# Taking a weight tile's scale from ScalarE's sums while VectorE inverts

## The chip, the cores and the metric

The kernel runs on one core of a Trainium2 chip. The metric is the device time of one execution in microseconds (us). Five engines of the core work side by side, each through its own queue in order: TensorE (PE, with weight loads as PEld), VectorE (DVE), ScalarE (ACT), GpSimd (POOL) and SyncE (SP, which issues most transfers).

## What is computed

One layer of a decoder trunk for a prompt of 1024 tokens and for 8 sample rows: an adaptive RMSNorm, one input projection of width 10368 from 2048 channels, two mixers and an output projection. The mixer that matters here is the RWKV-7 branch:

```
sa = S @ (-kk_t)
S  = S * d_t + sa * b_t + v_t * k_t        # for every token, per head of 64 channels
o  = S @ r_t
...
mixed = sigmoid(g_s5) * (o_s5 @ W_out[:D_S5]) + sigmoid(g_rw) * (o_rw @ W_out[D_S5:])
x = x + gate(c) * mixed
```

## The kernel before

**Products by jobs.** All large products are cut into jobs of 128 output channels (`run_jobs`). A job multiplies a weight tile of 2048 x 128 with the 1032 or 1040 columns of the activations, in three groups of some 344 columns. Operands are split into two float16 halves, a high and a low one, and three products of halves make one product, so a group is 3 x 16 = 48 matmuls (line 455) into one of three PSUM buffers `pg`. A group is read out by ACT and DVE: for a tile of the RWKV projections ACT writes a shifted copy `mt` (line 511) and DVE adds the two (line 517); for a gate branch `Z` the pair is lines 567 and 568. The buffer is free after DVE's part.

**Weight tiles.** Beside each job the next tile is prepared in three steps. `wload` fetches it as float32 into two buffers `ws` of 512 KB. `wscale` finds the largest magnitude: four searches of 128 x 512 each on DVE (`absmax`, the `wam` of line 157), a small one over their results (`wm`), a maximum over the partitions on POOL (`wg`), and five small DVE instructions that make a power of two of it (`wsc`, lines 147 to 151). `wsplit` then writes the high half `whi` on ACT (line 405) and the low half `wlo` on DVE (line 406), four times each. The fetch of the tile after next may start when the low halves are written.

**The recurrence.** The RWKV heads go in eight pairs (p = 0 to 7) through chunks of 64 tokens. For each pair `rw_operands` forms the chunk matrices, sends them through memory (`dA`), and `rw_tinv` inverts the 32 unit triangular matrices of a pair by elimination: 63 steps on DVE, each a product `TM` (line 800) and a subtraction that needs it (line 802). The results go to memory and back (`dT`, `TT`), and `rw_chain` walks over the 16 chunks with small matmuls on PE, the first of which that needs `TT` is `up` (line 835). `rw_side` transposes operands on DVE (line 770) and copies them on ACT (line 779).

**The order.** A hand-written planner (`Driver`) emits this background work between the matmuls of the jobs. Each generator yields its charge: nanoseconds of DVE, nanoseconds of PE, and a gap. The planner holds a clock for PE and one for DVE, and emits a step only while

```
b[1] <= self.pe and self.ve <= self.pe + self.slack
```

so what DVE is charged decides how many steps are emitted beside a job. A step of an inversion is charged `2 * (66 + n * m) / 0.96`, a search 600. Where a job needs a result, the planner is forced to emit up to it. The order of emission is a priority: a scheduler then lays instructions into the engines' queues, and sets later instructions between two that depend on each other.

PSUM buffers with the tag `pm` (two of them) serve the small products of the preparation, the tail and the operands; the inversions themselves use none.

Of the kernel before, what the change touches and what calls it, by code (L numbers as in the profile page):

```python
# [11 lines left out]
F32 = mybir.dt.float32  # L12
F16 = mybir.dt.float16
I32 = mybir.dt.int32
AF = mybir.ActivationFunctionType
# [51 lines left out]
class Driver:  # L67
# [6 lines left out]
    def __init__(self, slack=800.0):  # L74
        self.pe = 0.0
        self.ve = 0.0
        self.slack = slack
        self.bgs = []
# [52 lines left out]
class Hybrid:  # L131
    def __init__(self, ctx, tc, d):
        self.ctx, self.tc, self.nc, self.d = ctx, tc, tc.nc, d
        self.drv = Driver()
        self.scaled = False
        self.rotate = False
        self.flags = set()

# [236 lines left out]

    def wscale(self, job):

        n = len(job.ws)
        am = self.sm.tile([128, 4], F32, name="wam", tag="wam")
        for h in range(n):  # L380
            for q in range(2):
                self.absmax(am[:, 2 * h + q:2 * h + q + 1], job.ws[h][:, 4 * q:4 * q + 4, :], axis=mybir.AxisListType.XY)
                yield (600, 0, 0)
        m1 = self.sm.tile([128, 1], F32, name="wm1", tag="wm1")
        self.absmax(m1, am[:, :2 * n])
        g = self.sm.tile([128, 1], F32, name="wg", tag="wg")
        self.gmax(g, m1)
        yield (100, 0, WGAP)
        job.sc = self.sm.tile([128, 2, 1], F32, name="wsc", tag="wsc", bufs=3)
        self.pow2(g, job.sc)  # L390
        job.known = True
        yield (300, 0, 0)
# [398 lines left out]
    def rw_tinv(self, p):  # L791
        nc = self.nc
        TL = self.TL
        yield (0, 0, 5000)
        for k in range(63):
            n = k // 4 + 1
            m = 63 - k
            row = self.L1[:, k, k + 1:] if k < 32 else self.L2[:, k - 32, k - 31:]
            TM = self.TM[:, 0:n * m].rearrange("p (n m) -> p n m", m=m)
            nc.vector.tensor_tensor(out=TM, in0=row.unsqueeze(1).to_broadcast([128, n, m]),  # L800
                                    in1=TL[:, :n, k:k + 1].to_broadcast([128, n, m]), op=ALU.mult)
            nc.vector.tensor_tensor(out=TL[:, :n, k + 1:], in0=TL[:, :n, k + 1:], in1=TM, op=ALU.subtract)  # L802
            yield (2 * (66 + n * m) / 0.96, 0, 0)
        D4 = self.dT.rearrange("c h (j q) i -> q (c h) j i", q=4)
        for q in range(4):
            nc.sync.dma_start(D4[q], TL[32 * q:32 * q + 32])
        for e in range(2):
            for h in range(2):
                nc.sync.dma_start(self.TT[64 * e:64 * e + 64, :, 64 * h:64 * h + 64],
                                  self.dT[e::2, h].rearrange("c j i -> j c i"))  # L810
        yield (0, 0, 5500)
# [972 lines left out]
```

## Time and profile before

| | |
|---|---|
| median of 3 runs (lowest to highest) | 2981.96 us (2981.56 to 2985.08) |
| the profiled execution: its own time, its span | 2985.64 us, 2983.8 us |
| mean granted TensorE clock | 0.965 |
| PE busy, share of the span | 2726.1 us, 91% |
| DVE busy | 2031.8 us, 68% |
| ACT busy | 1102.7 us, 37% |
| DVE searches over weight tiles (`wam`) | 404, 267.7 us |

Busy time is the sum of an engine's instructions; it does not tell which of them the others waited for. The span is the time from the first to the last instruction. Matmuls overlap, so that one of them has a duration of some 0.31 us while a new one starts each 0.15 us.

### The profile page before, as it was taken

What the parts mean: (1) busy time and instruction counts of PE and PEld (TensorE: products, weight loads), DVE (VectorE), ACT (ScalarE), POOL (GpSimd) and SP (SyncE); (2) the same over time, 40 slices, a digit from 0 to 9 for tenths busy, and PEclk for the clock granted to TensorE, in tenths of its full rate; (3) what the DMA queues carried; (4) which work ended last, traced back from release to release, by engine and by line L of the source; (5) the groups of instructions that cost most, each with busy time, mean ns of one, the idle gap of its engine ahead of it and who ended that gap; (6) DMA issues with size and microseconds to landing.
All of it is one profiled execution on the core that took longest, in us unless ns stands there. A gap on an engine that the chain in (4) does not pass through costs nothing.

```text
span 2983.8 us, 47078 instructions
## 1 busy us (share of the span) xinstructions
PE 2726.1 (91%) x18330; PEld 1818.3 (61%) x18330; DVE 2031.8 (68%) x5106; ACT 1102.7 (37%) x1930; POOL 211.7 (7%) x426
## 2 busy tenths in 40 slices
PE   5699989999989999999899899999999897999997
PEld 1166656666656566666566566665666664666664
DVE  5579878754676756865857767667568855666665
ACT  2143223334434245254154253352442245522321
POOL 2100000010100100001001001000000000000002
PEclk7799999999999999999999999999999998999998
DMA  9734443331221222122212212222222347574443
GB/s 354 251 77 90 85 73 92 93 87 51 69 49 53 70 51 74 54 61 75 57 42 77 67 47 67 60 59 66 50 76 68 97 149 240 167 239 141 144 141 128
DMA packets 433582, 297.62 MB, mean 100 GB/s; under 512 B 115056, under 2 KB 399888, under 8 KB 432080
## 3 DMA queue, kind: packets, MB, share of 16 engines
q1 hardware_dynamic: 357136, 255.85, 30.5%
q10 hardware_dynamic: 76064, 38.47, 4.7%
q8 instruction: 144, 2.36, 0.3%
q14 instruction: 78, 0.64, 0.1%
q0 software_dynamic: 160, 0.30, 0.0%
HBM read 237.24 MB, written 57.32 MB: 99 GB/s over the span
## 4 chain that ended last, share of the span: by engine, by line
PE 28%; DVE 17%; DMA 10%; issue 6%; ACT 3%; POOL 1%; SPq 1%; ACTq 0%; DVEq 0%; POOLq 0%
PE pg L455 21%; DMA od<-BV 3%; DVE TM L800 3%; DVE ZB L802 3%; DMA ws<-w_in 3%; DVE wlo L406 2%; DVE wam L157 1%; PE pma L737 1%; DMA gw<-w_ada 1%; PE up L841 1%; PE sp L840 1%; DMA TT<-dT 1%; PE up L835 1%; PE xp L827 1%; PE xp L828 1%
## 5 line engine op out<-in xcount | busy, mean ns | idle before, releaser
L455 PEld LDWEIGHTS <-whi 128*128 128x128 f16 x9600 | 943.5, 99 | 550.2 <-issue 106.5
L455 PE MATMUL pg<-H,whi 128*128 128x344 f16 (+2 forms) x3840 | 1199.3, 312 | 60.9 <-DVE ZB L517 33.4
L455 PE MATMUL pg<-H,wlo 128*128 128x344 f16 (+2 forms) x3840 | 1199.4, 312 | 0.0
L455 PE MATMUL pg<-HL,whi 128*128 128x344 f16 (+2 forms) x3840 | 1199.1, 312 | 0.0
L455 PEld LDWEIGHTS <-wlo 128*128 128x128 f16 x4800 | 473.1, 99 | 236.7 <-issue 15.0
L405 ACT ACTIVATE whi<-ws,wsc 128x512 f16<-128x512 f32 x404 | 267.5, 713 | 374.7 <-PE pg L455 113.7
L157 DVE TENSOR_REDUCE wam<-ws 128x1 f32<-128x512 f32 x404 | 267.7, 679 | 146.8 <-DMA ws<-w_in 106.2
L406 DVE SCALAR_TENSOR_TENSOR wlo<-ws,wsc,whi 128x512 f16<-128x512 f32 x404 | 294.0, 748 | 42.1 <-ACT whi L405 40.6
L455 PE MATMUL pg<-OH,whi 128*128 128x344 f16 (+3 forms) x960 | 297.8, 311 | 10.4 <-ACT OH L1433 9.4
L455 PE MATMUL pg<-OLo,whi 128*128 128x344 f16 (+3 forms) x960 | 298.8, 311 | 4.0 <-DVE OLo L1435 2.7
L455 PE MATMUL pg<-OH,wlo 128*128 128x344 f16 (+3 forms) x960 | 298.8, 311 | 0.0
L800 DVE TENSOR_TENSOR TM<-ZB 128x252 f32<-128x252 f32 (+52 forms) x504 | 175.8, 349 | 78.4 <-DMA ZB<-dA 68.6
L802 DVE TENSOR_TENSOR ZB<-ZB,TM 128x252 f32<-128x252 f32 (+52 forms) x504 | 175.7, 349 | 10.2
L154 POOL PARTITION_ALL_REDUCE wg<-wm x105 | 47.1, 448 | 1459.4 <-DVE wm L157 1438.2
L236 PE MATMUL pmod<-wa,cs 128*32 128x512 f32 x256 | 76.2, 833 | 41.8 <-DMA wa<-w_ada 41.8
L830 ACT COPY XR<-xp 64x128 f32<-64x128 f32 x128 | 33.1, 259 | 219.7 <-DVE XS L829 219.2
L832 ACT ACTIVATE SG<-S,GC 128x128 f32<-128x128 f32 x120 | 48.0, 400 | 173.6 <-DVE S L843 134.5
L511 ACT ACTIVATE mt<-pg,rinv 128x347 f32<-128x347 f32 (+1 forms) x75 | 39.8, 538 | 139.0 <-PE pg L455 81.0
L835 PE MATMUL up<-XS,TT 128*128 128x128 f32 x256 | 56.3, 302 | 37.9 <-DMA TT<-dT 24.2
L1505 DVE SCALAR_TENSOR_TENSOR sg<-pg,oinv,sg 128x344 f32<-128x344 f32 (+3 forms) x96 | 54.9, 572 | 52.6 <-PE pg L455 52.4
L843 DVE SCALAR_TENSOR_TENSOR S<-sp,GC,SG 128x128 f32<-128x128 f32 x120 | 41.8, 348 | 69.5 <-PE sp L840 67.4
L701 ACT COPY BT<-ZB 64x128 f32<-64x128 f32 x256 | 75.7, 296 | 26.4 <-PE pma L737 17.6
(451 smaller groups left out, 3142.6 us busy)
## 6 DMA issues: line engine op xcount, KB each, us to landing
ws<-w_in SPq DMA_DIRECT2D x162, 512.0 KB
wa<-w_ada SPq DMA_DIRECT2D x64, 512.0 KB
sg<-sgd SPq DMA_DIRECT2D x32, 516.0 KB
gw<-w_ada ACTq DMA_DIRECT2D x32, 512.0 KB
ws<-w_out SPq DMA_DIRECT2D x32, 512.0 KB
XT<-xT SPq DMA_DIRECT2D x16, 516.0 KB
xo<-xT SPq DMA_DIRECT2D x16, 516.0 KB
ZB<-dA SPq DMA_DIRECT2D x8, 1024.0 KB
```

Source lines behind the costliest of these rows:

```text
L154: self.nc.gpsimd.partition_all_reduce(out, in_, 128, bass_isa.ReduceOp.absmax)
L157: self.nc.vector.tensor_reduce(out=out, in_=in_, axis=axis, op=ALU.max, apply_absolute_value=True)
L236: self.nc.tensor.matmul(q[s:s + 32], cs[:, kt, :], w[:, i, :], start=(kt < 4), stop=(kt >= 12))
L405: nc.scalar.activation(out=hi[:, ks, :], in_=s, func=AF.Copy, scale=job.sc[:, 0, 0:1])
L406: nc.vector.scalar_tensor_tensor(out=lo[:, ks, :], in0=s, scalar=job.sc[:, 0, 0:1], in1=hi[:, ks, :], op0=ALU.mult, op1=ALU.subtract)
L455: nc.tensor.matmul(q[:, :w], a[:, wk, :], b[:, rk, g0:g1], start=(n == 0), stop=(n == tot - 1))
L701: self.nc.scalar.copy(self.BT[k % 2][i][64 * h:64 * h + 64, :, 64 * h:64 * h + 64], t[64 * h:64 * h + 64, 128 * k:128 * k + 128].rearrange ...
L800: nc.vector.tensor_tensor(out=TM, in0=row.unsqueeze(1).to_broadcast([128, n, m]), in1=TL[:, :n, k:k + 1].to_broadcast([128, n, m]), op=ALU ...
L802: nc.vector.tensor_tensor(out=TL[:, :n, k + 1:], in0=TL[:, :n, k + 1:], in1=TM, op=ALU.subtract)
L832: nc.scalar.activation(out=self.SG, in_=S0, func=AF.Copy, scale=g)
L835: nc.tensor.matmul(up[:, 0, :], self.TT[:, a, :], xs, start=True, stop=True)
L1505: V.scalar_tensor_tensor(out=f, in0=q[:, :g1 - g0], scalar=job.inv[:, w:w + 1], in1=f, op0=ALU.mult, op1=ALU.mult)
```

## The change

While the 63 steps of an inversion are being emitted, a flag `inverting` is set. A weight tile whose `wscale` is emitted in that time no longer has its four searches on DVE. In their place stand four activations on ACT that write magnitudes to a PSUM buffer `pab`, which nobody reads, and whose accumulators give the sum of magnitudes along each row; the rest of the step goes on with sums in the place of maxima. The planner is charged 0 for them and not 600. Elsewhere the searches stay.

```
+        self.inverting = False
...
+                a, w = am[:, 2 * h + q:2 * h + q + 1], job.ws[h][:, 4 * q:4 * q + 4, :]
+                if self.inverting:
+
+                    o = self.ps.tile([128, 4, 128], F32, name="pab", tag="pm", bufs=2)
+                    nc.scalar.activation(out=o, in_=w, func=AF.Abs, accum_out=a)
+                    yield (0, 0, 0)
+                else:
+                    self.absmax(a, w, axis=mybir.AxisListType.XY)
+                    yield (600, 0, 0)
...
         yield (0, 0, 5000)
+        self.inverting = True
         for k in range(63):
...
             yield (2 * (66 + n * m) / 0.96, 0, 0)
+        self.inverting = False
```

## Rows read from the trace of the kernel before

**Rows 1.** The page's span, and part 1: busy time of each engine.

```profile
span 2983.8 us, 47078 instructions
PE 2726.1 (91%) x18330; PEld 1818.3 (61%) x18330; DVE 2031.8 (68%) x5106; ACT 1102.7 (37%) x1930; POOL 211.7 (7%) x426
```

**Rows 2.** Engines' busy us (and instructions): fifth inversion; sums over inversions; stretches after.

```profile
1606.00:1680.00 74.00, 67.81 (x453) 44.64 (x451) 64.06 (x187) 17.69 (x32) 6.79 (x16) 1.00 0.19 51
...
sum 582.00, PE 529.07 PEld 345.83 DVE 506.78 ACT 134.24 POOL 48.47; mean PE 66.13 PEld 43.23 DVE 63.35 ACT 16.78 POOL 6.06
...
sum 1066.00, PE 1006.32 PEld 703.04 DVE 647.63 ACT 501.61 POOL 68.25; mean PE 125.79 PEld 87.88 DVE 80.95 ACT 62.70 POOL 8.53
```

**Rows 3.** DVE's groups in the fifth inversion, 1606 to 1680 us.

```profile
L802 DVE TENSOR_TENSOR ZB<-ZB,TM 128x252 f32<-128x252 f32 (+52 forms) x63 | 21.9, 348 | 1.2
L800 DVE TENSOR_TENSOR TM<-ZB 128x252 f32<-128x252 f32 (+52 forms) x63 | 21.9, 348 | 8.6 <-DMA ZB<-dA 7.4
...
L157 DVE TENSOR_REDUCE wam<-ws 128x1 f32<-128x512 f32 x12 | 8.1, 678 | 0.9 <-DMA ws<-w_in 0.9
```

**Rows 4.** DVE in order of time, inside the fifth inversion.

```profile
1644.90 0.44 DVE L802 TENSOR_TENSOR ZB<-ZB,TM 128x280 f32<-128x280 f32 x1
1645.26 0.68 DVE L157 TENSOR_REDUCE wam<-ws 128x1 f32<-128x512 f32 x1
1645.86 0.43 DVE L800 TENSOR_TENSOR TM<-ZB 128x272 f32<-128x272 f32 x1
...
1650.37 0.44 DVE L800 TENSOR_TENSOR TM<-ZB 128x270 f32<-128x270 f32 x1
1650.84 0.44 DVE L802 TENSOR_TENSOR ZB<-ZB,TM 128x270 f32<-128x270 f32 x1
```

**Rows 5.** Instructions on `wam` between successive evacuations: length, DVE busy us (count), clock, DMA.

```profile
1625.69:1634.46 8.77, 0.00 (x0) 1.00 0.00 1
1634.46:1643.46 9.00, 0.69 (x1) 1.00 0.35 97
1643.46:1651.20 7.74, 2.19 (x4) 1.00 0.08 24
1651.20:1660.71 9.51, 0.00 (x0) 1.00 0.00 0
...
1668.07:1675.62 7.55, 1.50 (x3) 1.00 0.00 0
```

**Rows 6.** PE's waits over the whole span: in total, times, longest.

```profile
PE pg L455 <- DVE ZB L517: 33.4, 21, 2.3
PE up L835 <- DMA TT<-dT: 24.2, 6, 5.6
PE pg L455 <- DVE Z L568: 14.3, 11, 3.9
```

**Rows 7.** ACT's groups in the fifth inversion, 1606 to 1680 us.

```profile
L405 ACT ACTIVATE whi<-ws,wsc 128x512 f16<-128x512 f32 x8 | 5.3, 713 | 15.4 <-DVE rinv L499 15.4
...
L779 ACT COPY KN<-BV 32x512 f32<-32x512 f32 x5 | 3.1, 616 | 9.0 <-DVE BV L770 8.9
...
L830 ACT COPY XR<-xp 64x128 f32<-64x128 f32 x1 | 0.3, 261 | 14.9 <-DVE XS L829 14.9
L514 ACT ACTIVATE msh<-pg,rinv 128x8 f32<-128x8 f32 x1 | 0.3, 253 | 0.0
```

**Rows 8.** ACT's groups over the span, shapes kept apart.

```profile
L587 ACT ACT_TABLE_LOAD x39 | 50.0, 1283 | 18.8 <-DVE wsc L149 8.3 <-DMA sgd<-gt__10496 5.1 <-DMA sgd<-gt__12457 4.8
...
L869 ACT ACTIVATE pmq<-ON 128x512 f32<-128x512 f32 x16 | 9.5, 600 | 17.8 <-DVE M L742 10.1 <-DVE ON L865 6.7 <-DVE wsc L149 0.9
```

**Rows 9.** The two halves of one evacuation, in order of time.

```profile
1633.66 0.55 ACT L511 ACTIVATE mt<-pg,rinv 128x347 f32<-128x347 f32 x1 [6.51 <-PE pg L455]
...
1651.20 0.57 DVE L517 SCALAR_TENSOR_TENSOR ZB<-pg,rinv,mt 128x347 f32<-128x347 f32 x1
```

**Rows 10.** A piece of the chain that ended last: start, length, what.

```profile
1617.01 0.60 DVE wam L157
```

More of the change, by code (lines that the diff above doesn't have):

```diff
@@ L376, in wscale @@
     def wscale(self, job):
+        nc = self.nc
         n = len(job.ws)
@@ L381, in wscale @@
             for q in range(2):
-                self.absmax(am[:, 2 * h + q:2 * h + q + 1], job.ws[h][:, 4 * q:4 * q + 4, :], axis=mybir.AxisListType.XY)
-                yield (600, 0, 0)
+                a, w = am[:, 2 * h + q:2 * h + q + 1], job.ws[h][:, 4 * q:4 * q + 4, :]
[6 more added lines that the diff above has]
+                    yield (600, 0, 0)
         m1 = self.sm.tile([128, 1], F32, name="wm1", tag="wm1")
```

## The prediction

> **What bounds the kernel now.** I read the page first: the span and the engines' busy time [rows 1]. The reader is to see that PE is busy nine tenths of the time and DVE two thirds, so on average DVE isn't the bound. The second view is the busy time in stretches, each inversion by itself [rows 2]. In the fifth inversion DVE works 64.06 of 74 us while ACT works 17.69; over all eight PE is short of its span by 582 - 529.07 = 53 us, and in the stretches behind them, nearly twice as long, by 1066 - 1006.32 = 60 us. So an inversion is where PE is held most for its length, and DVE is full there. The third view is what fills DVE [rows 3]: 43.8 us of elimination, 8.1 us of searches on weight tiles (12 of them, three tiles), the rest low halves, evacuations and transposes. The others are alike: DVE works 506.78 of the 582 us of all eight [rows 2].
>
> Then DVE in order of time [rows 4]. A subtraction needs the product ahead of it, and the scheduler has set a search between the two. From the subtraction at 1644.90 to the product at 1645.86 it is 0.96 us with a search between, from 1650.37 to 1650.84 it is 0.47 us without. A search that lasts 0.68 us therefore costs the elimination 0.49 us, because its ends overlap its neighbours.
>
> The next view cuts the inversion at the DVE instructions that free a `pg` buffer [rows 5]; I show five of the seven stretches between the first such instruction and the last that I cut. PE fills one group in each, 48 matmuls that the planner charges with 0.146 us, 7.0 us. Where one search or none stands in a stretch it takes 8.77, 9.00 and 9.51 us and PE waits; where there are three or four instructions on `wam` (the small search over four results counts as one) it takes 7.55 to 7.74 us. The searches are not what makes DVE late: the steps are. The last view is PE's waits [rows 6]: 33.4 and 14.3 us on the two evacuations that stand mainly in inversions, about 6 us for each inversion, and 24.2 us on `TT`, the inverse that comes back from memory. Together that is the ceiling on what a lighter DVE could return there, some 72 us.
>
> **The change part by part.** *Which tiles.* The planner charges 33.0 us for the 63 steps (the sum of its formula) and 144 x 145.8 ns = 21.0 us for a job. With the preparation of the tiles at 5.3 us each, the copies of the side work and evacuations, an inversion is now emitted over some 58 us of the planner's PE clock, which holds the searches of up to three tiles. Without the charge of 2.4 us a tile the emission of the inversion ends 4.8 us earlier after two tiles, and the steps then left for the third tile's time are charged only 3.0 us. So I take two tiles an inversion, 8 searches, 64 in all; the bounds are 48 and 96.
>
> *What DVE loses.* 64 x 0.678 = 43 us of busy time [rows 3]; at its price between steps, 0.49 us [rows 4], 31 us, or 3.9 us an inversion. DVE's wait for the tile to arrive, 0.9 us in the fifth inversion [rows 3], goes with it in part, and comes back where `wm` waits for ACT.
>
> *What ACT gains.* 64 activations of 128 x 512 from SBUF to PSUM. The nearest row is the square of the same shape into PSUM, 0.600 us [rows 8]. What the accumulator's output costs no row shows: below nothing more, above the shortest activation on this engine, 0.253 us [rows 7]. I take 0.60 to 0.85 us, and 0.70 as value: 5.6 us an inversion on an engine that idles 56 of 74 us there [rows 2]. The instructions stand beside idle time and cost nothing as work; without that cover they would be 45 us.
>
> The Trainium skill ("ScalarE: Activation LUTs", section "Rules for kernel authors") gives a rule against the move: max, min and add belong on VectorE, which is the faster per element. By these rows the search takes 0.678 us on DVE and the square 0.600 us on ACT [rows 3, 8], so for float32 in this shape the trace disagrees. By the page the sum would be that ACT pays more than DVE saves; by the rows it pays about the same.
>
> *PSUM.* `pab` takes one of the two `pm` buffers for the length of an activation. In an inversion no matmul writes a `pm` tile, so nobody waits. Cost nothing; if the tail of the pair before still held both, one activation, 0.6 us, an inversion.
>
> *What the planner does with it.* This term decides. The charge that falls away is filled with steps of the elimination, because the planner emits up to its limit. It frees 8 x 0.6 = 4.8 us of charge an inversion, and the end of the inversion, `TT` and the chain stand 4.8 us earlier among PE's matmuls. DVE really frees 3.9 us (at 0.49) to 5.4 us (at 0.678), or 6.0 us with the tile's wait [rows 3]. PE's wait is the difference between what DVE needs and what PE was given to do meanwhile. It changes by 4.8 - 3.9 = +0.9 us at one end and by 4.8 - 6.0 = -1.2 us at the other. I take a value near the middle, -0.3 us, since not every search stands between two steps. The lateness itself stays: 63 steps take 43.8 us busy and 0.03 us between each two [rows 3, 4], 47.6 us, where 33.0 are charged.
>
> *The transfer behind an inversion* (`dT`, `TT`) is moved with the steps, past the same two fetches of weights in SP's queue; neither its DMAs nor their order behind the last step change. PE's 24.2 us on it [rows 6] stay.
>
> The sum: 8 x -0.3 = -2.4 us, and 0 for the rest, say -3 us; at the bounds -10 and +7. The profiled execution took 2985.64 us, 3.7 above the median, so it goes to 2983 there and 2979 as a median.
>
> **The rivals.** *The freed time reaches PE whole (faster).* If the evacuations keep their places between the same steps, every one comes 0.49 us earlier for each search ahead of it. Then PE's waits fall by 3.9 us an inversion, 31 us in all, and 43 us at the full price; with half of it, 16 us. For it: the chain that ended last runs through the searches, as the piece at 1617.01 [rows 10], and PE has 6 us of waits and then `TT` in each inversion to give back [rows 6]. Against: the order is laid out anew, and stretches with searches are the fast ones [rows 5]. Its time is 2982 - 16 = 2966, from 2951 to 2976.
>
> *DVE waits for ACT (slower).* `wm` stays on DVE and now needs the fourth activation. Behind `wm` in DVE's queue stand the steps and the evacuations, and PE waits for those. ACT is idle but not free: in the fifth inversion it stands 15.4 us at `whi`, 8.9 us at the copies of `KN` and 14.9 us at `XR`, each time for DVE [rows 7]. An activation queued behind one of these is late by what is left of that wait. The point from which it decides is 4 x 0.49 = 2.0 us of DVE wait at `wm` for each tile; four activations of 0.70 us after the tile has come are 2.8 us already, of which the other work of DVE covers some. With 3.0 us of wait a tile the loss is 16 x 1.0 = 16 us, 2998. Against: ACT runs ahead of DVE there. The first half of an evacuation starts at 1633.66 and the second at 1651.20 [rows 9], so ACT has 17 us in hand at that place.
>
> *A table load for Abs (slower).* A load takes 1.283 us [rows 8]. With one before and one after each tile, 16 x 2.57 = 41 us lie on ACT ahead of `wm`, and DVE would wait beyond the point above: about 3020. No load stands among ACT's groups of the fifth inversion, where Sigmoid and copies alternate. The Trainium skill ("ScalarE: Activation LUTs", section "Table sets: the hidden batching unit") states that abs is in every set; the rows so far agree only for copies.
>
> *It does less than it says.* With one tile an inversion, or none, the result is that of the forecast, 2980 to 2982.
>
> **How the numbers follow.** About 0.2%, 6 us, is what a measurement of this kernel can tell from no change. The forecast (within 6 us, the few tiles included) has 0.38. The freed time reaching PE, by 7 us or more, has 0.37: a ceiling of 72 us of PE waits stands behind it. DVE waiting for ACT, or an order of instructions that comes out worse, has 0.23, the table load 0.02. The likeliest case by itself lies between 2972 and 2989, its bounds. The range reaches to the middle of the faster rival, with its full price left out, and to the slower one without its far end: 2957 to 2995. That leaves out about 1 in 10 at either side.
>
> **What would show it.** On DVE the `wam` searches fall from 404 to about 340, and on ACT some 64 activations write `pab` at 0.60 to 0.85 us, with no more table loads than before. An inversion shortens by 4 to 6 us, from 73 to about 68. PE's waits on the two evacuations and on `TT` stay within 10 us of 72 in sum; this is the step that decides. If they fall by 20 us or more the first rival holds. If DVE shows a wait of `wm` on ACT of more than 2 us a tile the second holds. The prediction is wrong above all if the order of evacuations against steps isn't shifted as the planner's charges say.

## The result, and the profile after

The changed kernel took 3003.39 us (median of 4 runs, 2998.29 to 3007.69) beside 2983.52 us of the kernel before (4 runs, 2981.56 to 2988.06). The ratio is 1.0064, interval 1.0043 to 1.0084: slower by some 19 us by the ratio, outside the range forecast. The profiled execution took 3007.69 us, 4.3 above the median.

The page's span and busy times of the changed kernel, which answer to [rows 1]:

```profile
span 3005.8 us, 47196 instructions
...
PE 2743.7 (91%) x18330; PEld 1818.3 (60%) x18330; DVE 2008.1 (67%) x5042; ACT 1137.2 (38%) x2057; POOL 214.6 (7%) x426
```

The instructions on the tile `pab` of the changed kernel (shortest, median and longest in ns, first and last start in us), and under them its DVE searches:

```profile
L388 ACT ACTIVATE pab<-ws x64: 574/588/602, 779.6 to 2272.2; 128x512 f32<-128x512 f32 x64
L388 ACT ACTIVATION_READ_ACCUMULATOR pab<-ws x64: 185/187/203, 780.2 to 2272.7; 128x1 f32 x64
...
L158 DVE TENSOR_REDUCE wam<-ws x340: 660/678/690, 31.8 to 2929.4; 128x1 f32<-128x512 f32 x170
```

The reader is to see that 64 searches moved, as forecast, and that a sum is two instructions on ACT, 0.59 and 0.19 us.

The changed kernel's windows over the inversions, the fifth and the sum of all eight, with the columns of [rows 2]:

```profile
1621.00:1688.70 67.70, 56.91 (x350) 36.48 (x349) 59.72 (x181) 14.76 (x30) 4.05 (x8) 0.90 0.19 51
...
sum 542.10, PE 463.64 PEld 300.87 DVE 474.15 ACT 134.39 POOL 31.51; mean PE 57.95 PEld 37.61 DVE 59.27 ACT 16.80 POOL 3.94
```

These windows run from the first step of an inversion to its last; those of [rows 2] are cut at whole us. Cut as here, the eight inversions of the kernel before are:

```profile
sum 578.80, PE 526.87 PEld 344.36 DVE 506.44 ACT 130.65 POOL 48.47; mean PE 65.86 PEld 43.04 DVE 63.31 ACT 16.33 POOL 6.06
```

So they are now 578.8 - 542.1 = 36.7 us shorter, 4.6 each, and DVE works 506.44 - 474.15 = 32.3 us less in them, 4.0 each. But PE is now short of their length by 542.1 - 463.64 = 78.5 us where it was 51.9. In the fifth its granted clock is 0.90; it was 1.00.

ACT's instructions on `pab` in the same windows, the fifth and the sum (length; busy us and count; clock; DMA share; GB/s):

```profile
1621.00:1688.70 67.70, 2.67 (x8) 0.90 0.19 51
...
sum 542.10, ACT 24.32; mean ACT 3.04
```

A sum and its reading are two instructions, so four sums, one tile, ran inside the fifth inversion. Over all eight it is 36 of the 64. The other 28 ran 12 to 22 us ahead of the first step of an inversion: the flag follows the planner's emission, and DVE begins the steps later than that.

PE's waits in the changed kernel, over the span (total, times, longest), for [rows 6]:

```profile
PE xp L839 <- DVE BV L795: 43.4, 5, 14.3
...
PE pma L746 <- ACT BT L710: 13.1, 17, 1.4
PE up L846 <- DMA TT<-dT: 12.5, 3, 7.7
...
PE pg L464 <- DVE Z L577: 10.4, 7, 2.3
PE pg L464 <- DVE ZB L526: 9.2, 6, 2.3
```

The two evacuations and `TT` fell from 71.9 to 32.1 us. In their place stands a wait that the list of before does not have: 43.4 us of the chain's first matmul, `xp`, for DVE's product `BV`. `xp` is written to the PSUM buffer in which `rw_side` leaves a part of `pmb`, and that buffer is free when DVE has read it. With this wait the sum is 75.5 us, not far from the 71.9 of before.

The longest of these waits, in the fourth inversion: PE, then DVE, in order of time, then windows around it (length; busy us and count of PE, PEld, DVE, ACT, POOL; clock; DMA share; GB/s):

```profile
1420.18 1.90 PE L794 MATMUL pmb<-ZB,c_mat 128*128 128x344 f32 x6
...
1425.52 0.31 PE L464 MATMUL pg<-H,whi 128*128 128x347 f16 x1
1440.09 0.76 PE L839 MATMUL xp<-VN,M 128*128 128x128 f32 x2 [14.25 <-DVE BV L795]
1440.64 0.50 PE L464 MATMUL pg<-HL,whi 128*128 128x347 f16 x1
```

```profile
1437.31 0.42 DVE L812 TENSOR_TENSOR ZB<-ZB,TM 128x253 f32<-128x253 f32 x1
...
1439.43 0.51 DVE L795 TENSOR_TENSOR BV<-pmb,ZB 128x344 f32<-128x344 f32 x1
```

```profile
1418.00:1425.50 7.50, 6.26 (x38) 4.01 (x36) 6.46 (x17) 0.00 (x0) 0.51 (x1) 1.00 0.34 97
1425.50:1440.10 14.60, 0.35 (x4) 0.05 (x1) 13.91 (x39) 2.99 (x5) 0.30 (x1) 0.61 0.00 0
1440.10:1445.90 5.80, 5.80 (x21) 3.56 (x22) 5.73 (x15) 0.26 (x1) 0.28 (x1) 0.50 0.31 85
```

PE made `pmb` at 1420.18; DVE read it at 1439.43, after steps of the elimination that stood ahead of it in its queue. PE did nothing for 14.25 us. Behind the wait the granted clock is 0.50, the lower level (1.2 GHz), for 5.8 us of full work: the same weight matmul takes 0.50 us in the records there and 0.31 ahead of the wait.

DVE's waits in the changed kernel, from 790 to 2330 us:

```profile
DVE TM L810 <- DMA ZB<-dA: 80.9, 8, 13.7
...
DVE wm L158 <- ACT pab L388: 44.5, 11, 7.1
...
DVE p2m L148 <- POOL wg L155: 18.0, 45, 1.5
```

So the second rival's wait is there too: 44.5 us over 16 tiles, 2.8 us a tile, past its point of 2.0. Some 25 us of it lie outside the inversions, at the tiles that were summed ahead of them.

One more view adds up where the time went: one window from the first weight matmul of the job in which the recurrence begins (774.2 us before, 780.7 after) to the last weight matmul of the kernel. PE runs 14,022 recorded matmuls in it in both. The kernel before, then the changed kernel:

```profile
774.20:2963.00 2188.80, 2049.57 (x14022) 1390.75 (x14021) 1474.65 (x3797) 831.42 (x1505) 137.57 (x315) 0.98 0.32 90
780.70:2985.00 2204.30, 2063.53 (x14022) 1388.71 (x14021) 1451.78 (x3744) 865.82 (x1631) 140.28 (x316) 0.97 0.32 90
```

Of the 15.5 us more, PE's idle time is 1.5 (140.8 less 139.2) and its busy time 14.0, for the same matmuls. The other 6.5 us between the two profiles lie ahead of the recurrence, where the programs do the same: the kernel of e5 below, alike up to there, begins at 774.0.

### The profile page after: what moved, and what is told of

It reads as the page before. It is cut to its first block, busy times and chain, and to the rows that moved or that the text cites. A ratio compares the mean times of both kernels' runs of the same rounds, so it can differ in the third digit from the quotient of the medians.

```text
span 3005.8 us, 47196 instructions
## 1 busy us (share of the span) xinstructions
PE 2743.7 (91%) x18330; PEld 1818.3 (60%) x18330; DVE 2008.1 (67%) x5042; ACT 1137.2 (38%) x2057; POOL 214.6 (7%) x426
## 4 chain that ended last, share of the span: by engine, by line
PE 45%; DVE 24%; DMA 18%; ACT 7%; issue 4%; POOL 1%; SPq 1%; ACTq 0%; DVEq 0%; POOLq 0%
PE pg L464 32%; DMA ws<-w_in 8%; DVE wlo L415 3%; DVE ZB L812 3%; DVE TM L810 3%; DMA ZB<-dA 2%; DVE wam L158 2%; DMA wa<-w_ada 2%; PE sp L851 1%; DMA od<-BV 1%; PE up L852 1%; PE up L846 1%; ACT BT L710 1%; PE pmod L237 1%; PE pma L746 1%
## 5 line engine op out<-in xcount | busy, mean ns | idle before, releaser
L158 DVE TENSOR_REDUCE wam<-ws 128x1 f32<-128x512 f32 x340 | 224.7, 679 | 156.6 <-DMA ws<-w_in 97.1
L810 DVE TENSOR_TENSOR TM<-ZB 128x252 f32<-128x252 f32 (+52 forms) x504 | 178.1, 353 | 91.7 <-DMA ZB<-dA 80.9
L237 PE MATMUL pmod<-wa,cs 128*32 128x512 f32 x256 | 75.9, 850 | 44.5 <-DMA wa<-w_ada 36.3
L839 PE MATMUL xp<-VN,M 128*128 128x128 f32 x256 | 51.9, 286 | 43.4 <-DVE BV L795 43.4
L746 PE MATMUL pma<-AR,BT 128*128 128x128 f32 x512 | 72.1, 283 | 17.9 <-ACT BT L710 13.1
```

The lines of the kernel that those rows point to most:

```text
L158: self.nc.vector.tensor_reduce(out=out, in_=in_, axis=axis, op=ALU.max, apply_absolute_value=True)
L237: self.nc.tensor.matmul(q[s:s + 32], cs[:, kt, :], w[:, i, :], start=(kt < 4), stop=(kt >= 12))
L746: nc.tensor.matmul(q[:, e, 128 * i:128 * i + 128], w[:, e, :], self.AR[:, a, 128 * e:128 * e + 128], start=True, stop=True)
L839: nc.tensor.matmul(xp, mk, self.VN[:, k, :], start=(k == 0), stop=True)
```

## The experiments

Eighteen kernels ran, each timed beside the kernel before (medians there 2971.5 to 2974.0 us). Each is told by its edit against the changed kernel, if nothing else is said. The last two columns are the window just described, of one profiled execution each; the profiled execution of the kernel before took 2985.64 us, 0.4% over its medians here, and that of e3 2984.24, 10 us over e3's own median, so a difference of 10 us in the window's length tells little.

| run | searches in an inversion | charge, ns | further edit | ratio (interval) | window, us | PE idle, us |
|---|---|---|---|---|---|---|
| before | VectorE | 600 | | 1 | 2188.8 | 139.2 |
| changed | ScalarE, 64 | 0 | | 1.0064 (1.0043 to 1.0084) | 2204.3 | 140.8 |
| e1 | ScalarE, 88 | 600 | | 0.9951 (0.9932 to 0.9969) | 2163.6 | 117.3 |
| e2 | VectorE | 0 | | 1.0052 (1.0032 to 1.0072) | 2187.9 | 129.0 |
| e3 | none | 0 | | 1.0016 (1.0001 to 1.0031) | 2177.5 | 124.6 |
| e4 | none | 600 | | 0.9983 (0.9966 to 1.0001) | 2167.3 | 119.2 |
| e5 | ScalarE, 64 | 0 | `pmb` on tag pm | 1.0123 (1.0100 to 1.0146) | 2212.7 | 157.0 |
| e6 | ScalarE, 72 | 300 | | 0.9993 (0.9976 to 1.0011) | 2178.2 | 125.4 |
| e7 | VectorE | 600 | steps charged higher | 1.0139 (1.0115 to 1.0163) | 2216.9 | 169.7 |
| e8 | ScalarE, 76 | 1200 | | 0.9986 (0.9972 to 1.0000) | 2177.2 | 133.6 |
| e9 | ScalarE, 64 | 0 | ScalarE reads `pmb` | 1.0039 (1.0026 to 1.0051) | 2187.5 | 122.9 |
| e10 | ScalarE, 72 | 0 | chain held back | 0.9963 (0.9949 to 0.9978) | 2164.2 | 124.5 |
| e11 | ScalarE, 308 | 600 | all later tiles | 0.9897 (0.9877 to 0.9917) | 2142.7 | 98.1 |
| e12 | VectorE | 0 | chain held back | 1.0044 (1.0028 to 1.0060) | 2185.0 | 134.2 |
| e13 | ScalarE, 60 | 0 | gap ahead of `wm` | 1.0033 (1.0016 to 1.0049) | 2191.0 | 130.9 |
| e14 | ScalarE, 60 | 0 | e9 and e13 | 1.0031 (1.0018 to 1.0044) | 2187.3 | 126.6 |
| e15 | ScalarE, 308 | 600 | e11 and e13 | 0.9998 (0.9986 to 1.0010) | 2170.0 | 124.9 |
| e16 | ScalarE, 64 | 0 | `wm` on GpSimd | 1.0005 (0.9992 to 1.0019) | 2174.7 | 122.7 |
| e17 | ScalarE, 64 | 0 | e9 and e16 | 0.9937 (0.9919 to 0.9954) | 2153.1 | 106.1 |
| e18 | ScalarE, 308 | 600 | e11 and e16 | 1.0215 (1.0196 to 1.0235) | 2239.7 | 175.6 |

### The engine or the charge (e1 to e4)

The change has two parts: the engine, and the charge of 600 ns of VectorE that falls away. e1 restores the charge:

```diff
-                    yield (0, 0, 0)
+                    yield (600, 0, 0)
```

> The sums stay on ScalarE, but the planner is charged 600 for each again, so the emission is that of the kernel before. If the missing charge is what costs (the emission of an inversion's end moves up and TensorE meets the chain's first matmul too early), the wait of xp on BV, 43.4 us after the change, is gone and the time is 2975 to 2986 us. If the move to ScalarE itself costs (tile waits on ScalarE, 75.8 us, and wm behind them on VectorE, 44.5 us), it stays at 2995 to 3005 us.

e2 leaves the searches on VectorE and takes only the charge away:

```diff
-                    o = self.ps.tile([128, 4, 128], F32, name="pab", tag="pm", bufs=2)
-                    nc.scalar.activation(out=o, in_=w, func=AF.Abs, accum_out=a)
+                    self.absmax(a, w, axis=mybir.AxisListType.XY)
```

> The searches stay on VectorE, but the planner is charged 0 for them while an inversion is emitted. If the missing charge costs, this is as slow as the changed kernel or slower, 3000 to 3015 us, since VectorE's work isn't even lighter, and xp waits on BV again for over 30 us. If the move to ScalarE costs, it is 2980 to 2990 us.

e3 and e4 (the same with charge 600) put `nc.gpsimd.memset(a, 0.2)` in the place of the sum: the tile isn't read, and its power of two comes from a constant.

> Neither engine reads the tile: GpSimd sets the row results to the constant 0.2, so that the scale of these tiles no longer follows from their weights; charge 0. Shows what a lighter VectorE is worth without any wait on ScalarE. If the missing charge costs, 2995 to 3010 us with xp waiting on BV; if ScalarE's waits cost, 2960 to 2980 us.

> As the one before (the row results are set to 0.2 and the tile isn't read), with the charge of 600 kept. If freed time on VectorE reaches TensorE whole when the emission doesn't move, 2945 to 2965 us; if it goes where TensorE doesn't wait, 2975 to 2985 us.

The ranges were stated on a kernel of 2982 us. On it the ratios of e1 to e4 make 2967, 2997, 2987 and 2977 us: e1 is below its ranges, e2 and e3 lie between their two, and only e4 is inside one, the one in which freed time goes where TensorE doesn't wait.

With the charge, the move makes the kernel faster (0.9951); without it, the kernel is slower whichever engine searches (1.0064, 1.0052). The missing charge costs in all three pairs: 0.5 parts in a hundred where VectorE searches, 1.1 with the sums on ScalarE, 0.3 where nobody reads the tile. So the move to ScalarE by itself isn't what costs; the missing charge is. But without the charge the sums do cost something: the changed kernel is 0.5 above e3. PE's main wait in e3:

```profile
PE xp L838 <- DVE BV L794: 42.5, 5, 12.9
```

That is the wait of the changed kernel (43.4 us), with a ratio of 1.0016. So this wait by itself does not make the loss. PE's waits in e1:

```profile
PE up L846 <- DMA TT<-dT: 32.8, 7, 5.4
PE pg L464 <- DVE ZB L526: 31.2, 18, 2.5
...
PE pg L464 <- DVE Z L577: 8.8, 8, 1.8
```

They are those of [rows 6], 72.8 us in sum, with no wait of `xp` on `BV`, and DVE waits 6.4 us at `wm`. Emitted over a longer stretch, the inversions took in 88 sums, not 64, so e1 differs from the changed kernel by these 24 too. Nor does DVE's relief alone explain e1: e4 takes as many searches off DVE (88), with the same charge and with 73.0 us in these three waits, and has 0.9983. Why e1 is faster than e4 is open.

### The shared buffer (e5, e9)

e5 takes `pmb` off the chain's buffers:

```diff
-                q = self.ps.tile([128, 512], F32, name="pmb", tag=tag)
+                q = self.ps.tile([128, 512], F32, name="pmb", tag="pm", bufs=2)
```

> The changed kernel, charge 0, with the three PSUM tiles of rw_side (pmb) taken from the tag pm (two buffers) and no longer from xp, sp and up, which the chain's matmuls use. Theory A (without the charge the chain's first matmul is queued in the middle of the inversion and TensorE then stands at the one buffer that pmb holds until VectorE reads it): the wait of xp on the product BV, 43 us in the profile of the changed kernel, is gone; TensorE's waits in the five inversions fall by at least half of it, and the ratio to the kernel before comes to 0.985 to 0.999. Theory B (the order itself is at fault: with the chain's first steps so early TensorE must wait for the inversion's end in any case): another wait of like length stands in its place, at the inverse TT or at the products pma, and the ratio stays at 1.003 to 1.009.

PE's longest wait in e5:

```profile
PE pmb L794 <- DVE BV L795: 80.3, 7, 14.9
```

The wait at `xp` went, and a greater one came: three parts of `pmb` share two buffers, so the third waits until DVE has read the first. Another wait stood in its place, as Theory B had it, but at `pmb` and nearly twice as long, and 1.0123 is above both ranges. e9 frees the buffer without DVE:

```diff
-                V.tensor_tensor(out=self.BV[:, g0:g1], in0=q[:, :g1 - g0], in1=Vv[:, g0:g1], op=ALU.mult)
+                nc.scalar.copy(self.BV[:, g0:g1], q[:, :g1 - g0])
+                V.tensor_tensor(out=self.BV[:, g0:g1], in0=self.BV[:, g0:g1], in1=Vv[:, g0:g1], op=ALU.mult)
```

> The changed kernel, charge 0, with pmb read out of PSUM by ScalarE (three copies of 128x344 a pair, some 0.55 us each by the like copies of pml) and the product BV made by VectorE from SBUF, so that xp's buffer comes free without VectorE. Theory A (TensorE's wait at xp is all there is to the loss): the wait of xp on BV is gone, what stands in its place is under a third of its 43 us, the granted clock's loss in the five inversions falls with it, and the ratio is 0.990 to 1.001. Theory B (TensorE runs ahead of VectorE by the missing charge and stands at whichever buffer comes next): waits at TT, XS, M or pma grow by two thirds of the 43 us or more, and the ratio stays at 1.003 to 1.010.

PE's waits in e9:

```profile
PE up L847 <- DMA TT<-dT: 22.5, 7, 7.0
PE pg L464 <- DVE ZB L526: 20.7, 13, 2.3
...
PE pg L464 <- DVE Z L577: 14.9, 12, 3.0
```

The wait at `xp` is gone, and these three are 58.1 us where the changed kernel has 32.1: 26 of the 43 us came back elsewhere, between what the two theories said. The ratio, 1.0039, is in Theory B's range and gives back 0.25 of 0.64 parts in a hundred. PE's busy time in the window did not fall with the wait: 2187.5 - 122.9 = 2064.6 us, where the changed kernel has 2063.5 and the kernel before 2049.6.

### How much charge, and where (e6 to e8)

e6 and e8 set the charge behind a sum to 300 and to 1200 ns. e7 is the kernel before with the inversion's steps charged nearer to their real length:

```diff
-            yield (2 * (66 + n * m) / 0.96, 0, 0)
+            yield (2 * (145 + n * m) / 0.96, 0, 0)
```

> The changed kernel with a charge of 300 ns of VectorE behind each of the 64 sums in place of 0 (and of the 600 of the run that was faster). Theory A (how early the chain's first matmul is queued decides, by steps of a whole matmul group): between the two, 0.995 to 1.007, and the share follows the place of the first xp in TensorE's queue; where it stands past 5 groups there is no wait at BV. Theory B (the 600 is only one order among many that happen to differ by some us): a value outside of the two, below 0.993 or above 1.009.

> The changed kernel with a charge of 1200 ns behind each of the 64 sums, twice that of the faster run. Theory A (more charge puts the chain later and nearer to when VectorE is truly done): 0.985 to 0.997, TensorE's wait at the inverse TT below the 32.8 us of the run with 600. Theory B (600 is already enough to keep xp behind BV, and what more adds only delays the last pair): 0.996 to 1.006, the stretch from the last inversion to the output longer by up to 10 us.

> The kernel before, VectorE's searches unchanged, with a greater charge for the 63 double steps of an inversion: 2 * (145 + n * m) / 0.96 in place of 2 * (66 + n * m) / 0.96, 10.4 us more an inversion, 43.4 in place of 33.0 us, with 47.6 us of real busy time. Theory A (a charge below the real time lets the planner put the end of the inversion too early in TensorE's queue, and each us taken off it makes this worse, so one put on makes it better): faster, 0.985 to 0.997, with less of TensorE's wait at the inverse TT (24.2 us before). Theory B (the charge of before is near the best; more delays the chain, whose end then runs into the output products): 1.000 to 1.010, with longer waits at jobs behind the last inversion.

300 ns gives a value between 0 and 600 (0.9993), with 32.4 us of wait at `xp`, in three inversions. Counted in groups of 48 weight matmuls from the inversion's start, the first `xp` stands at 5.9, 5.5, 4.2, 3.4 and 3.2 in the third to seventh inversions there, where the kernel before has 6.7 to 6.9: it slides forward from pair to pair. The wait is there from the fifth on, and at 5.9 and 5.5 groups it isn't, as Theory A had it. 1200 ns is not better than 600 (0.9986, in Theory B's range): a wait of 41.3 us at `ZB` and 20.4 at `TT`. e7 took 1.0139, above both ranges. It does not test whether later is better, since the chain did not come later there: in the fifth inversion its first `xp` stands behind 188 weight matmuls, 3.9 groups. PE's main wait in e7, then the ACT instruction behind which it stands:

```profile
PE pml L651 <- ACT ZB L652: 67.1, 7, 11.4
```

```profile
1713.51 1.16 ACT L661 ACTIVATE ZB<-ZB,c_vec 128x1032 f32<-128x1032 f32 x1 [18.72 <-DVE TM L800]
```

PE's part of the next pair's preparation (`pml`) now begins inside each of the first seven inversions, where in the kernel before it does so in the first alone. One of ACT's activations for it waits 18.72 us for the elimination's last steps, and every evacuation behind it on ACT waits with it. So of the four charges of a sum 600 is the best, and too little and too much, on the sums or on the steps, fail at different places.

### Holding the chain back (e10, e12)

e10 leaves the charge at 0 and delays the chain alone:

```diff
-        yield (0, 0, 5500)
+        yield (0, 0, 30500)
```

> The changed kernel, charge 0, with the planner's gap between the end of an inversion and the chain's first step raised from 5500 to 30500 ns, about three more groups of weight matmuls of 8.3 us. Theory A (the chain queued too early, in TensorE's order, is what costs; the inversion's own steps may be early): first xp back at 6 to 7 groups behind the inversion's start, no wait at BV, ratio 0.990 to 1.000. Theory B (the lost charge costs by the early steps of the inversion and of what stands before it): TensorE waits as long at another place, 1.003 to 1.010; theory C (the chain is now late and its end delays the next pair and the output): the stretch behind the last inversion is longer by 20 us or more, 1.002 to 1.012.

The busy time of PE on `pg` from the fourth inversion's start to its first `xp`, and in brackets the matmuls, 48 to a group, in the kernel before, the changed kernel and e10:

```profile
1398.40:1456.60 58.20, 49.51 (x321) 3.62 (x7) 4.48 (x9) 0.97 0.21 54
```

```profile
1390.90:1440.10 49.20, 27.26 (x174) 1.71 (x3) 2.66 (x5) 0.85 0.15 47
```

```profile
1389.70:1447.90 58.20, 49.16 (x329) 4.21 (x8) 3.89 (x8) 1.00 0.19 58
```

Without the charge `xp` stood behind 174 weight matmuls, not 321: three groups earlier in PE's queue. The gap put it back, no `xp` waits for `BV`, and the ratio is 0.9963, with the charge still 0, as Theory A had it. DVE's wait at `wm` fell as well, to 10.3 us, so this run does not part the two waits. e12 is the control: the same gap, with the searches on VectorE (e2).

> The searches on VectorE as before, but charge 0 behind each of those emitted in an inversion, and the chain held back by the gap of 30500 ns: the control for the run with the sums on ScalarE, charge 0 and the same gap (0.9963). Theory A (the gap only undoes the early chain, and what made that run faster than the kernel before is VectorE's relief): 0.999 to 1.003, with 0.3% to 0.7% between the two, and TensorE's waits at ZB, Z and TT no shorter than before. Theory B (the gap is the gain, and the relief is worth nothing): 0.994 to 0.998.

It took 1.0044, where both theories had put it lower: with VectorE searching, the gap repairs next to nothing. The gap took the wait at `xp` away here too, but 30.7 us at `TT`, 35.9 at `ZB` and 15.0 at `Z` stood in its place. Between e12 and e10 lies the move alone, 0.8%; between the kernel before and e1 it is 0.5%; between e2 and the changed kernel, nothing.

### VectorE's wait for ScalarE (e13, e14, e16, e17)

e13 puts a gap ahead of the search over the four results, e14 adds the edit of e9:

```diff
+        if self.inverting:
+            yield (0, 0, 8000)
         m1 = self.sm.tile([128, 1], F32, name="wm1", tag="wm1")
```

> The changed kernel, charge 0, with a gap of 8000 ns of the planner's time between the fourth sum and the search over the four results, so that steps of the elimination stand in VectorE's queue ahead of wm. Theory A (two waits make up the loss: VectorE at wm for ScalarE, 44.5 us, and TensorE at xp, 43.4 us; with charge 0 the four sums and wm are queued with nothing between them): the wait at wm falls below 15 us, that at xp stays, and the ratio is 1.000 to 1.004, as in the run without any sums and without the charge (1.0016). Theory B (VectorE's wait at wm lies beside TensorE's own and costs nothing): 1.005 to 1.008 with the wait gone all the same.

> The same gap ahead of wm, and pmb read out by ScalarE as in the run that took TensorE's wait at xp away (1.0039). Theory A (the two waits add up): both are gone and the ratio is 0.997 to 1.002. Theory B (one of them hides the other, or other waits take their place): no better than the better of the two single edits, 1.001 to 1.005.

The gap missed its aim: DVE waits 44.9 us at `wm` in e13 and 52.8 in e14. The ratios (1.0033, 1.0031) lie in ranges of Theory A and of Theory B, but with the wait still there they say nothing about it. e16 takes the search off DVE's queue, and e17 adds the edit of e9. The power of two comes from the sum of the four results there, not from the greatest:

```diff
+        if self.inverting:
+            nc.gpsimd.tensor_tensor(out=am[:, :n], in0=am[:, :n], in1=am[:, n:2 * n], op=ALU.add)
+            nc.gpsimd.tensor_tensor(out=m1, in0=am[:, 0:1], in1=am[:, n - 1:n], op=ALU.add)
+        else:
+            self.absmax(m1, am[:, :2 * n])
-        self.absmax(m1, am[:, :2 * n])
```

> The changed kernel, charge 0, with the search over the four results (wm) of a tile in an inversion taken from VectorE and given to GpSimd, as two small additions (the power of two then comes from the sum of the four results and not from their greatest). GpSimd then waits for ScalarE's sums and VectorE doesn't. Theory A (VectorE's wait at wm, 44.5 us, is the other part of the loss): that wait is gone, no like wait takes its place on VectorE, and the ratio is 0.999 to 1.003. Theory B (it costs nothing, since VectorE waits instead at the power of two, one step later, or since TensorE stands at xp in any case): 1.004 to 1.008.

> The same, and pmb read out by ScalarE (1.0039 by itself). Theory A (both waits add up to most of the loss): 0.994 to 1.000. Theory B: 1.002 to 1.006.

e16 takes 0.59 parts in a hundred off, e9 took 0.25, both together 1.27: 0.9937, better than either, and more than the sum of the two. DVE's waits in e16, from 790 to 2300 us:

```profile
DVE p2m L148 <- POOL wg L155: 80.6, 43, 15.2
...
DVE TM L814 <- DMA ZB<-dA: 45.3, 8, 9.7
```

The wait did not vanish: DVE now stands at the power of two, one step later. Together with the wait for the product's rows (`dA`) it is 125.9 us, where the changed kernel has 44.5 + 18.0 + 80.9 = 143.4. What comes in front of it in DVE's queue can be done by then, and PE's wait at `xp` is 28.4 us, not 43.4; against that, PE waits 21.3 us for `whi`. So the ratio is in Theory A's range without its condition.

PE's waits for `pmb` in e17:

```profile
PE sp L854 <- ACT BV L799: 19.9, 3, 7.2
...
PE xp L844 <- ACT BV L799: 4.6, 1, 4.6
```

These are 24.5 us, now for ACT's copies and mainly at a later matmul of the chain, and DVE waits 83.8 us at the power of two. So neither wait is gone in the fastest of these kernels, and no run shows what makes it fast.

### More sums on ScalarE (e11, e15, e18)

e11 is e1 with the flag left set, so that ScalarE sums every weight tile from the first inversion on:

```diff
-        self.inverting = False
         D4 = self.dT.rearrange("c h (j q) i -> q (c h) j i", q=4)
```

> The run with charge 600 that was faster, with the sums of magnitudes on ScalarE for every weight tile from the first inversion on, not in the inversions alone. Theory A (relief of VectorE pays where VectorE is full, in the inversions, and there it has been had): within 0.3% of that run, 0.992 to 0.998. Theory B (relief pays wherever evacuations queue on VectorE): 0.985 to 0.992. Theory C (ScalarE's evacuations stand behind the sums, which wait for the weights' transfers): 0.998 to 1.010.

It is the fastest: 0.9897, 2938.50 us beside 2973.91, in Theory B's range. Its page:

```profile
PE 2725.5 (93%) x18330; PEld 1821.2 (62%) x18330; DVE 1861.7 (63%) x4798; ACT 1303.4 (44%) x2548; POOL 212.2 (7%) x426
```

308 sums moved. DVE works 170 us less than in the kernel before, ACT 201 more, and PE's idle time in the window is 98.1 us. e15 and e18 add the edits of e13 and e16:

> The fastest version so far (0.9897: charge 600, sums on ScalarE for all weight tiles from the first inversion on) with the same gap ahead of wm; VectorE waits 57.6 us there at wm for ScalarE, 38 times. Theory A (that wait costs): 0.983 to 0.988. Theory B (it lies where VectorE has time, and a later power of two delays the halves of the weights): 0.989 to 0.996.

> The fastest version (0.9897) with the search over the four results on GpSimd for every tile from the first inversion on; VectorE waited 57.6 us there at wm. Theory A: 0.981 to 0.987. Theory B: 0.988 to 0.992.

Both are above all their ranges: e15 gives the gain back, and e18 is slower than the kernel before by 2%. In e15 DVE's wait at `wm` grew from 57.6 to 146.3 us, and `xp` waits for `BV` again, 22.5 us. In e18 GpSimd stands in its queue for the sums, and the halves of the weights come late. Waits of GpSimd, then of PE, in e18:

```profile
POOL wam L395 <- ACT pab L388: 583.5, 38, 53.6
```

```profile
PE pg L468 <- ACT whi L418: 92.4, 15, 13.1
```

## Why the prediction was wrong

*Which tiles, what DVE loses, what ACT gains.* In number these held. 64 searches moved, an inversion shortened by 4.6 us (4 to 6 forecast), DVE's work in it fell by 4.0 us (3.9 by the price between steps). But 28 of the sums ran ahead of the inversions, so that one tile was taken from most inversions and not two. DVE's busy time over the span fell by 23.7 us, where 43 and 31 stood. A sum takes 0.59 us and a reading of 0.19 us on ACT: 0.78 where 0.70 was taken. A slip in the reading of [rows 4] changes no term: the search shown there stands between a subtraction and the next product, not between a product and its subtraction.

*PSUM.* No wait of PE names `pab`. That no matmul writes a `pm` tile in an inversion doesn't hold for the first one, which has four of `pml`. And `pmb`, which the prediction did not look at, holds buffers that DVE must free, and there PE came to stand.

*The transfer.* PE's wait at `TT` did not stay: it fell from 24.2 to 12.5 us. In e9, where PE waits 0.9 us at `xp`, it is 22.5, so PE had done most of this waiting at `xp`.

*What the planner does with it.* This is the step that failed. It had the freed charge refilled, the chain 4.8 us earlier among PE's matmuls, and PE's old waits changed by -0.3 us an inversion. The chain came earlier not by 4.8 us but by three groups of 7.0 us in the fourth inversion. In the second to seventh inversions the first `xp` stands at 5.1, 4.6, 3.6, 2.8, 3.3 and 2.9 groups, where the kernel before has 6.1 and then 6.7 to 6.9: the lead grows from pair to pair up to the fifth and then stays. That each inversion's gain in the planner's time was added to the next one's is inferred from this slide and from that of the 300 ns run. And the waits of [rows 6] did not stay within 10 us of 72: they fell by 40, by which the text would have had the first rival hold. Another wait of 43 us took their place. The net of PE's idle time, +1.5 us where -2.4 stood in the sum, came near by chance.

The sum had no term for PE's busy time, which rose by 14.0 us for the same matmuls. In the window 206 weight matmuls have more than 0.4 us, against 150 before; at 0.146 us more each that is some 8 us, an estimate from the two traces. The rest stays open. It isn't the price of the wait at `xp`: e9 has the busy time without the wait, and e3, with 42.5 us of the wait, has PE busy for 2177.5 - 124.6 = 2052.9 us. Nor had the sum a term for DVE's stand at `wm`.

*The sizes hidden in it.* The forecast set two great terms against each other as one small one. Read from the runs, the move with its charge is worth -0.5% (0.9951), and the missing charge +1.1% (1.0064 over 0.9951), of which some belongs to the 24 sums that e1 has more.

*The freed time reaches PE whole.* By its number this fits e1: 0.49% of 2979 is 15 us, the half gain that this rival priced at 16. By its mechanism it isn't shown: e4 frees DVE of as many searches with the same charge and gains 0.17%, 5 us.

*DVE waits for ACT.* Its condition came true, 2.8 us a tile against 2.0, and its 2998 us is the nearest of the times given. Of its two reasons, an ACT held up by its own waits for DVE is not the one seen: ACT stands 4.3 us for DVE at `pab`. The other is: ACT stands there 75.8 us for the tiles, and four sums then take 4 x 0.78 = 3.1 us. With charge 0 the four sums and `wm` are emitted with no step between them, and nothing covers that; with the charge of 600 the wait is 6.4 us in 22 tiles. e3 and e16 bear it out as a cause: without a wait at `wm`, and with 42.5 and 28.4 us still at `xp`, they have 1.0016 and 1.0005. That in e16 the wait moved to the power of two leaves open how.

*A table load.* It did not come with the sums: the profile's rows of loads add up to 112, beside 113 before, and to 115 in e11. The Trainium skill ("ScalarE: Activation LUTs", section "Table sets: the hidden batching unit") has abs in every set; this case's trace agrees for 64 and for 308 activations.

*The rule against the move.* The Trainium skill ("ScalarE: Activation LUTs", section "Rules for kernel authors") gives max to VectorE and states its lead, up to about 3 times, for bf16. The prediction left the type out, so its float32 rows could not disagree with that lead. Per instruction the search is ahead in float32 too, 0.68 us against 0.59 + 0.19. The kernel with 308 sums on ScalarE is 1% faster all the same, with 170 us less of work on DVE.

So the loss is a matter of the planner's charge and the order that it makes. Three pairs show the charge (before and e2, e1 and the changed kernel, e4 and e3), and with the sums on ScalarE holding the chain back repairs it as well (e10, 0.9963). Which wait passes it on is shown only in part: taking away the one at `xp` (e9) or the one at `wm` (e16) gives some back, and e17 gives all back with 24.5 us for `pmb` and 83.8 us at the power of two still there. Open are why the gap of e12 gives so little where VectorE searches, and why e1 is faster than e4. No run shows how far the time moves by an edit of the order that should be neutral, so differences of some 0.3% between two kernels may be the order alone.

## What to carry to other kernels

A cost in a hand-made planner is not only an account of an engine's time; it sets where everything behind it stands in every queue. Move work to another engine with its charge left in place first, and change the charge as an edit of its own. When a removed wait should give time back, look along the critical engine's queue for the buffer at which it would stand next, and for who frees it.

## What the hardware showed that was not expected

The accumulator's output of an activation is an instruction of its own on ACT, 185 to 203 ns, which the row of a plain activation doesn't show. And a wait of PE can cost more than its length: after the 14.25 us at `xp` the granted clock stayed at 0.50 through 5.8 us of full work, and weight matmuls took 0.50 us in place of 0.31 in the records.
